# Column tiles for the recurrence's chunk products, whole rows for the sample's

## The chip, the cores and the metric

The kernel runs on one core of one Trainium2 chip. The core has a matrix engine (TensorE, PE in the profile, with PEld its weight loads), three others that compute (VectorE or DVE, ScalarE or ACT, GpSimd or POOL) and an engine that issues DMAs (SyncE or SP). The metric is the device time of one execution in microseconds (us), lower is better. Every product of two matrices reads a stationary operand (the weights) that is loaded into TensorE's array of 128 rows by 128 columns, and a moving operand that streams past it; a shape such as 128*32 in the profile names the rows and columns of the array that a product uses.

## The reference, cut to what matters

One layer of a streaming encoder over 2048 prompt frames and 64 frames of a running stream (the sample). Half of the width is chunked attention (8 heads of 64), half a gated linear recurrence, HGRN2 (4 heads of 128); each half is gated, both are joined, projected, added to the input and normalised.

```python
aq, ak, av, ag, hq, hf, hi, hg = jnp.split(rms_norm(x, ln_g) @ w_in, SPLITS, axis=-1)
o_a = attn_fn(heads(aq), k, v).reshape(B, T, W_A) * jax.nn.silu(ag)
o_b, S = hgrn2_branch(hq, hf, hi, hg, lb, norm_g, s0)
y = x + jnp.concatenate([o_a, o_b], axis=-1) @ w_out
```

The recurrence works by blocks. With b the running sum of the logarithms of the forget gates:

```python
qt = qb * jnp.exp(b)
kt = kb * jnp.exp(-b)
A = jnp.where(mask, jnp.einsum('bthk,bshk->bhts', qt, kt), 0.0)
o = jnp.einsum('bthk,bhkv->bthv', qt, S) + jnp.einsum('bhts,bshv->bthv', A, vb)
S = jnp.exp(bl)[..., None] * S + jnp.einsum('bshk,bshv->bhkv', kb * jnp.exp(bl[:, None] - b), vb)
```

Everything is float32; the outputs are both streams' results, the newest keys and values, and the recurrence's states.

## The kernel before, in words

The frames are worked off in four super-blocks of 512 columns; the second has 576, the last 64 of them the sample (SUPER, L38). For each super-block TensorE projects 32 groups of 128 features from the normalised input (project, L539; results in PSUM tiles `acc`, weights in `w`). Four of eight kinds of groups feed four pairs of attention heads (pair_jobs, L759), four feed four recurrence heads (head_jobs, L1248).

The order of the instructions on all engines is written out by a planner at build time (class Plan, L52). Each piece of work is a thread that yields what it waits for: a time, a token for a buffer (Tok), or a condition. The planner keeps a clock, C.now, which every product advances by an assumed cost (L132: 10 + 1.66 n ns for an fp32 product of n moving columns, marked slow); the other engines have a time at which they are free. The main thread emits the projections, two products at a time; between them whatever thread is ready emits its instructions. The engines then run their own instructions in that order and wait for one another by semaphores. All transfers are issued by SP.

**The recurrence** (rec_block, L1362) takes a block of a head's columns: 512, or in the second super-block first 256 and then 320, so there are 12 blocks of four chunks of 128 columns, four of two chunks, and four of two chunks and a sample chunk of 64. A chunk consists of blocks of 32 columns. Exponentials scale queries and keys relative to the middle of their block of 32 (q0, k0), to its start or end (q1, k1), or to the middle of the chunk (q2, k2), so that each is in range. The products inside a chunk (L1497 to L1508) write one PSUM tile `g`, keys by queries: k0 with q0, 128 by 128, which is right on the diagonal blocks of 32; then k1 of blocks 0 and 2 with q1 of blocks 1 and 3, 32 by 32; then k2 of blocks 0 and 1 with q2 of blocks 2 and 3, 64 by 64. Later ones overwrite what is not wanted of the earlier ones. VectorE copies what the mask keeps into `asb` (L1513), whose other entries stay zero. After that come the state update (kv, L1545: turned keys kn with the values iv), the states (L1567, L1569), and the output (og, L1580: iv with A, and the state before with qh, L1583). The sample's chunk has 64 rows, so those products use 64 rows of iv, kn and A. The products are fp32; TensorE executes each as two records.

**The sample's attention** (sample_a, L1161): five blocks of keys, four from the cache (vc) and one of 64 new ones (v); the probabilities of both heads are turned and split into two parts (split_p, L976: ScalarE copies, VectorE subtracts) in tiles `ph`, and ten products write `pv`. The tile `v` holds two heads, nine blocks of 128 keys; block 8 is the sample's, 64 rows of it used.

**The last pair's values** (ev_v_last, L835, in the last super-block): the projected values are turned by TensorE for each head of the pair, four transposes of 64 rows each, once that head's half of `v` is open (open_, L772; a half opens when the pair before has ended with it).

Of the kernel before, what the change touches and what calls it, by code (L numbers as in the profile page):

```python
# [17 lines left out]
P = 128  # L18
# [3 lines left out]
DEC = 64  # L22
# [161 lines left out]
def hymba_step(  # L184
# [574 lines left out]
    def pair_jobs(sb, p):  # L759
# [12 lines left out]
        def open_(h):  # L772

            yield from tk[f"kv{h}"].get()
            if "kd" not in room:
                room["kd"] = T(pa, [P, 2, WIN + NMAX], F32R, "kd")
                room["v"] = T(pa, [P, 2, 9, 2, 64], F32R, "v")
                room["q"] = T(pa, [P, 2, QW], F32R, "q")
            d.kd, d.v, d.q = room["kd"], room["v"], room["q"]
            if sb:  # L780
                cd = carry[sb - 1][p]
                sp.dma_start(f32(d.kd[:, h, 0:512]), cd[:, h])
                d.k_t[h] = C.dma(256)
                sp.dma_start(f32(d.v[:, h, 0:4].rearrange("p t s d -> p (t s d)")), cd[:, 2 + h])
                d.v_t[h] = C.dma(256)
            d.open[h] = True
            C.spawn(load_bias(sb, p, d, h), 1)
# [47 lines left out]
        def ev_v_last(acc, off, bn, t):  # L835
            yield from tk["vT"].get()
            yield "A", t
            vt = T(wk, [P, 512], F32, "vT", bufs=VTB)
            act.copy(vt[:, :bn], acc)
            t = C.act(bn, t)  # L840
            tk["acc"].put(1, t)
            nt = bn // P
            for h in range(2):
                yield lambda: d.open[h]
                yield from tk["tr"].get()
                yield t
                pt = tr_ps()
                for j in range(nt):
                    transpose(pt[:, j * 64 : j * 64 + 64], vt[own[h], j * P : (j + 1) * P], ident[own[h], own[h]])
                yield "A", C.pe()  # L850
                s3 = pt[:, : nt * 64].rearrange("p (t d) -> p t d", d=64)
                hi, lo = (d.v[:, h, 4 + off // P : 4 + off // P + nt, x] for x in (h, 1 - h))
                act.copy(hi, s3)
                t = C.act(nt * 64)
                yield "D", t
                dve.tensor_sub(lo, s3, f32(hi))
                t = C.dve(nt * 64, t)
                tk["tr"].put(1, t)
                d.v_n[h] += bn
                d.v_t[h] = max(d.v_t[h], t + 500.0)  # L860
            yield from new_rows(vt, off, bn, p, nv_prompt, None, tk["vT"], t)
            all_in()

# [297 lines left out]
    def sample_a(d, c0, marks):  # L1161
        yield lambda: d.left == [1, 1]
        yield lambda: d.cache is not None and all(x >= c0 + DEC for x in d.q_n + d.k_n + d.v_n)
        yield "D", max(d.q_t + d.k_t + d.v_t)
        q, kd, v, p = d.q, d.kd, d.v, d.p
        kc, vc = d.cache


        spans = [(kc, 0, 512), (kd, 512 + c0, DEC)]

        z = c0 + DEC
        for part in (q, ql):
            dve.memset(f32(part[:, :, z : z + DEC]), 0.0)
            dve.tensor_copy(part[:, 1, z + DEC : z + 2 * DEC], f32(part[:, 1, c0:z]))
        t = C.dve(500)
        yield t
        yield from tk["s_ps"].get()
        yield from tk["pr"].get()
        sps = s_ps()
        for i, (ks, k0, kn) in enumerate(spans):  # L1180
            for part in (q, ql):
                for h in range(2):
                    a = (c0, z)[h]
                    mm(sps[:, i, :kn], part[:, h, a : a + P], ks[:, h, k0 : k0 + kn], kn,
                       start=part is q and h == 0, stop=part is ql and h == 1)
        t = C.pe()
        yield "D", t
        s = T(wk, [P, 640], F32, "pr", bufs=PRB)
        nm = T(wk, [P, 2], F32, "nm", bufs=4)
        for h in range(2):  # L1190
            hs = own[h]
            for i, kn in enumerate((512, DEC)):
                dve.tensor_tensor_reduce(s[hs, i * 512 : i * 512 + kn], sps[hs, i, :kn],
                                         d.bias[hs, h, 64 * h + i * 512 : 64 * h + i * 512 + kn],
                                         1.0, 3e38, ALU.add, ALU.min, nm[hs, i : i + 1])
                t = C.dve(kn, t)
        dve.tensor_tensor(nm[:, 0:1], nm[:, 0:1], nm[:, 1:2], ALU.min)
        t = C.dve(10, t)
        tk["s_ps"].put(1, t)
        for h in range(2):  # L1200
            d.left[h] -= 1
            tk[f"bias{h}"].put()
        yield "A", t
        out = []
        yield from softmax_exp(s, nm, 576, out, t)
        pr, t = out[0]
        yield lambda: marks[-1]["pv"] and turn["ph"] == turn["given"]
        yield t + 300.0
        phs = []
        for j0, nj, kr in ((0, 4, P), (4, 1, DEC)):  # L1210
            yield from tk["tr"].get()
            pt = tr_ps()
            for j in range(j0, j0 + nj):
                transpose(pt[:kr, (j - j0) * P : (j - j0 + 1) * P], pr[:, j * P : j * P + kr], ident)
            t = C.pe()
            if j0:
                tk["pr"].put(1, t)
            yield "A", t
            yield from tk["ph"].get()
            ph = T(wk, [P, 2, 512], F32R, "ph", bufs=2)  # L1220
            t = yield from split_p(pt, ph, kr, nj * P, t)
            tk["tr"].put(1, t)
            phs.append(ph)
        yield t + 200.0
        yield from tk["mixa"].get()
        mix = T(wk, [P, 256], F32, "mixa", bufs=2)
        yield from tk["pv"].get()
        pv = psum("pv").rearrange("p (h s q) -> p h s q", h=2, s=2)[:, :, :, :DEC]
        for h in range(2):
            for j in range(5):  # L1230
                kr = P if j < 4 else DEC
                cc = (j % 4) * P + h * DEC
                mm(pv[:, h], vcols(vc, j, h, kr) if j < 4 else vcols(v, 4 + c0 // P, h, kr), phs[j // 4][:kr, :, cc : cc + DEC], P,
                   start=(j == 0), stop=(j == 4))
        tk["ph"].put(2, C.pe())
        t = C.pe()
        yield "A", t
        for h in range(2):
            t = yield from finish_pv(h, pv[:, h], mix, DEC, t)
        tk["pv"].put(1, t)  # L1240
        tk["raw"].put(2)
        C.spawn(mix_out(d, mix, c0, DEC, t, True), 1)
# [5 lines left out]
    def head_jobs(sb, h):  # L1248
# [65 lines left out]
        def ifree():  # L1314
            if r.gi is None:
                if tk["gi"].n == 0:
                    return False
                tk["gi"].take()
                r.gi = True
                r.iv = T(pg, [P, 5 * P], F32, "gi")  # L1320
            return True

        def qd():
# [26 lines left out]
    def recurrence(r):  # L1350
        sb, h = r.sb, r.h
        t0, n, blocks = SUPER[sb][:3]
        for bi, (off, bn) in enumerate(blocks):
# [4 lines left out]
            yield from rec_block(r, off, bn, lastb)  # L1358
            tk["rec"].put()
        tk["gi"].put()  # L1360

    def rec_block(r, off, bn, lastb):  # L1362
        sb, h = r.sb, r.h
# [130 lines left out]
        yield td  # L1494
        yield from tk["g"].get()
        ag = bank()
        for i, (cc, nbk, smp) in enumerate(chunks):  # L1497
            w = nbk * 32
            mm(ag[:w, i, :w], k0[:, cc : cc + w], q0[:, cc : cc + w], w, True, start=True, stop=True)
        yield None  # L1500
        for i, (cc, nbk, smp) in enumerate(chunks):
            for j in range(0, nbk, 2):
                a, b = cc + 32 * j, cc + 32 * j + 32
                mm(ag[32 * j : 32 * j + 32, i, 32 * j + 32 : 32 * j + 64],
                   k1[:, a : a + 32], q1[:, b : b + 32], 32, start=True, stop=True)
        for i in range(nprc):
            mm(ag[0:64, i, 64:128], k2[:, i].rearrange("p j t -> p (j t)"),
               q2[:, i].rearrange("p j t -> p (j t)"), 150, start=True, stop=True)  # L1508
        t = C.pe()
        yield "D", t  # L1510
        for cs, w in merged():
# [4 lines left out]
        if by_dma:  # L1516
# [6 lines left out]
                         kh[:, :full].rearrange("p (a c j) -> p c a j", a=4, j=32))  # L1523
            if bn > full:
                act.copy(kn[:DEC, nprc], kh[:DEC, full : full + P])
            t = C.act(bn, rows["t"])
            yield t + 200.0
        else:
# [7 lines left out]
            kn = tmp("k1").rearrange("p (c t) -> p c t", t=P)  # L1536
            for cs, w in merged():
                act.copy(kn[:w, cs], tg[:w, cs])
            t = C.act(bn, t)
            yield t + 200.0  # L1540
        kv = bank()
        iv = r.iv
        for i, (cc, nbk, smp) in enumerate(chunks):
            w = nbk * 32
            mm(kv[:, i], kn[:w, i], iv[:w, off + cc : off + cc + P], P, True, start=True, stop=True)  # L1545
        t = C.pe()
        yield "D", t
        before = []
# [28 lines left out]
        og = bank()  # L1577
        for i, (cc, nbk, smp) in enumerate(chunks):
            w = nbk * 32
            mm(og[:, i, :w], iv[:w, off + cc : off + cc + P], A[:w, i, :w], P, True,  # L1580
               start=True, stop=before[i] is None)
            if before[i] is not None:
                mm(og[:, i, :w], before[i], qh[:, cc : cc + w], P, True, start=False, stop=True)  # L1583
# [673 lines left out]
```

## Time and profile before

| | |
|---|---|
| median of 3 runs | 1241.81 us (1240.01 to 1243.0) |
| the profiled execution's own time | 1241.93 us |
| its span in the profile | 1240.2 us |
| TensorE busy | 1228.5 us (99%), 7398 records |
| VectorE, ScalarE, GpSimd busy | 893.8, 680.3, 417.3 us |
| granted clock of TensorE | 0.999 |

A row of a group names line, engine, operation, tiles (out<-in), shape, count, then busy time and the mean duration of one, then idle time before it. A row of the timeline has the start in us, the time from the first start to the last end of the merged instructions, and their count; where instructions of several shapes of one line and the same tiles follow one another, one row holds them all under the first one's shape. A window's rows hold the records that fall into it. A matmul's duration is a latency, and records overlap; the distance of starts tells what one costs.

### The profile page before, as it was taken

Reading aid. Unit: us, or ns where it says so; the run is one execution under the profiler, and the core shown is the slowest. Engines: PE = TensorE matmul, PEld = TensorE weight load, DVE = VectorE, ACT = ScalarE, POOL = GpSimd, SP = SyncE. Lnnn points to the kernel's source line nnn. Section 1 sums busy time; section 2 is a strip of 40 time slices with the busy share of each in tenths; the row PEclk is TensorE's granted clock in tenths of the full one; section 3 lists DMA queues with packets and bytes.
Section 4 is the critical chain, followed back from the end, with each engine's and each line's share of the span. In section 5 each row is a group of like instructions: output and inputs, shape, how many; then the busy total and the mean of one; then the engine's idle time right before and its main releaser. Section 6 shows DMA issues by size and latency. Waiting matters only on the chain.

```text
span 1240.2 us, 21233 instructions
## 1 busy us (share of the span) xinstructions
PE 1228.5 (99%) x7398; PEld 1078.9 (87%) x7398; DVE 893.8 (72%) x1897; ACT 680.3 (55%) x1526; POOL 417.3 (34%) x702
## 2 busy tenths in 40 slices
PE   9999999999999999999999999999999999999997
PEld 7888888999999999998888888988888888788786
DVE  7687878777767677687587667785768566867775
ACT  6354546655565547574465556664646445644443
POOL 7665565111120111201242242133342202665543
PEclk9999999999999999999999999999999999999999
DMA  8897979667575476555787878678888686988431
GB/s 339 302 319 256 328 281 343 205 179 242 159 221 156 150 238 210 193 167 187 265 270 253 300 241 282 227 238 276 261 275 262 222 251 212 336 260 252 131 136 68
DMA packets 158324, 294.36 MB, mean 237 GB/s; under 512 B 51657, under 2 KB 98377, under 8 KB 140554
## 3 DMA queue, kind: packets, MB, share of 16 engines
q1 hardware_dynamic: 157784, 292.74, 70.7%
q8 instruction: 58, 0.95, 0.3%
q14 instruction: 48, 0.39, 0.1%
q10 hardware_dynamic: 434, 0.27, 0.1%
HBM read 198.52 MB, written 95.49 MB: 237 GB/s over the span
## 4 chain that ended last, share of the span: by engine, by line
PE 90%; DMA 5%; DVE 2%; ACT 1%; SPq 1%; issue 0%; POOL 0%; ACTq 0%; DVEq 0%; POOLq 0%
PE acc L249 58%; PE g L249 9%; PE pv L249 7%; PE tr L253 6%; PE s L249 5%; PE tr L249 4%; DMA vT<-way 2%; DMA w<-wd 2%; DMA way<-vT 1%; DMA out_dram<-ck 1%; PE g L253 1%; DMA bias<-wind 0%; DVE pr L948 0%; SPq L711 0%; SPq L1684 0%
## 5 line engine op out<-in xcount | busy, mean ns | idle before, releaser
L249 PE MATMUL acc<-xh,w 128*128 128x512 f32 (+2 forms) x2720 | 564.5, 347 | 0.6 <-ACT xh L409 0.5
L249 PEld LDWEIGHTS acc<-xh,w 128*128 128x128 f32 x2720 | 435.7, 189 | 51.5 <-ACT xh L409 0.9
L249 PE MATMUL acc<-xl,w 128*128 128x512 f32 (+2 forms) x1360 | 291.4, 346 | 0.2 <-DVE xl L415 0.2
L249 PEld LDWEIGHTS acc<-xl,w 128*128 128x128 f32 x1360 | 220.5, 189 | 26.2 <-DVE xl L415 0.4
L948 DVE CUSTOM_DVE_ANT_0 pr<-s,bias 128x640 f32<-128x640 f32 (+4 forms) x128 | 94.2, 736 | 53.6 <-PE s L249 53.1
L965 ACT ACTIVATE pr<-pr,nm 128x640 f32<-128x640 f32 (+4 forms) x132 | 100.3, 760 | 52.8 <-DVE nm L948 52.5
L977 ACT CAST ph<-tr 128x512 fp32r<-128x512 f32 (+3 forms) x176 | 87.8, 506 | 74.5 <-PE pv L249 45.5
L473 POOL TENSOR_TENSOR w<-wraw,w 128x256 fp32r<-128x256 f32 x120 | 102.3, 881 | 55.6 <-DVE w L468 40.5
L980 DVE TENSOR_TENSOR ph<-tr,ph 128x512 fp32r<-128x512 f32 (+3 forms) x176 | 100.7, 587 | 21.6 <-ACT ph L977 21.0
L249 PE MATMUL pv<-ph,v 128*128 128x256 f32 (+2 forms) x344 | 97.8, 371 | 0.9 <-DVE ph L980 0.6
L253 PE MATMUL tr<-ident,pr 128*128 128x128 f32 x580 | 88.2, 273 | 0.5 <-DVE sm L968 0.5
L1596 POOL TENSOR_TENSOR k<-ob 128x512 f32<-128x512 f32 (+2 forms) x20 | 18.0, 902 | 200.3 <-ACT ob L1587 162.3
L510 POOL TENSOR_TENSOR xn<-wraw,xn 128x256 fp32r<-128x256 f32 x48 | 40.6, 848 | 132.1 <-ACT xn L507 127.1
L1121 POOL TENSOR_TENSOR mixa<-mixa,sga 128x256 f32<-128x256 f32 (+1 forms) x36 | 28.6, 793 | 167.9 <-DVE mixa L1019 142.2
L969 DVE TENSOR_SCALAR pr<-pr,sm 128x640 f32<-128x640 f32 (+4 forms) x132 | 76.2, 577 | 4.7
L1019 DVE TENSOR_TENSOR mixa<-mixa,pv 64x256 f32<-64x256 f32 (+1 forms) x144 | 56.8, 394 | 31.0 <-ACT mixa L1015 27.3
L253 PEld LDWEIGHTS tr<-ident,pr 128*128 128x128 f32 x580 | 69.8, 140 | 10.3 <-PE tr L253 0.9
L575 ACT ACTIVATE sig<-acc 128x512 f32<-128x512 f32 (+2 forms) x63 | 31.8, 505 | 72.8 <-PE acc L249 72.1
L249 PEld LDWEIGHTS pv<-ph,v 128*128 128x128 f32 (+1 forms) x344 | 58.2, 189 | 9.8 <-DVE ph L980 1.4
L1015 ACT COPY mixa<-pv 64x256 f32<-64x256 f32 (+1 forms) x72 | 25.1, 349 | 59.4 <-PE pv L249 53.3
L249 PE MATMUL s<-kd,q 128*128 128x320 f32 (+2 forms) x232 | 55.8, 311 | 0.2 <-DVE nm L948 0.2
L249 PE MATMUL s<-kd,ql 128*128 128x320 f32 (+2 forms) x232 | 55.5, 309 | 0.0
(415 smaller groups left out, 2122.5 us busy)
## 6 DMA issues: line engine op xcount, KB each, us to landing
w<-wd SPq DMA_DIRECT2D x96, 1024.0 KB, 5.8
wd<-w SPq DMA_DIRECT2D x32, 1024.0 KB, 7.4
wraw<-in_w_in_dram SPq DMA_DIRECT2D x30, 512.0 KB, 5.4
wod<-xn SPq DMA_DIRECT2D x28, 512.0 KB, 5.8
xn<-in_x_prompt_dram SPq DMA_DIRECT2D x23, 512.0 KB, 4.8
bias<-biasd SPq DMA_DIRECT2D x24, 320.0 KB, 5.5
carry<-kd SPq DMA_DIRECT2D x12, 512.0 KB, 6.2
carry<-v SPq DMA_DIRECT2D x12, 512.0 KB, 6.4
```

The source lines that it names most:

```text
L249: pe.matmul(out, w, x, **kw)
L253: pe.transpose(out, x, idn)
L473: pool.tensor_sub(w[:, 1, k : k + 2], raw[:, k : k + 2], f32(w[:, 0, k : k + 2]))
L510: pool.tensor_sub(f32r(st[:, c.start + 512 : c.stop + 512]), src[:, c], st[:, c])
L575: act.activation(sig[:, :bn], acc, AF.Exp, scale=-1.0)
L948: dve.tensor_tensor_reduce(s[:, :nk].rearrange("p (a c) -> p a c", a=ns), sps[:, :ns, :kn], d.bias[:, h, bcol : bcol + nk].rearrange("p (a ...
L965: act.activation(s[:, :nk], s[:, :nk], AF.Exp, bias=nm[:, 0:1], scale=-1.0, accum_out=sm)
L969: dve.tensor_scalar(s[:, :nk], s[:, :nk], sm, None, ALU.mult)
L977: act.copy(ph[:krows, 0, :wid], pt[:krows, :wid])
L980: dve.tensor_sub(ph[:krows, 1, :wid], pt[:krows, :wid], f32(ph[:krows, 0, :wid]))
L1019: dve.tensor_add(mix[hs, :qn], mix[hs, :qn], pv[hs, i, :qn])
L1121: pool.tensor_mul(mix[:, :n], mix[:, :n], d.sg[:, g0 : g0 + n])
```

## The change

The products inside a chunk are all made 32 columns of the array wide (block_mm), at the array's columns where their 32 rows of output lie. The product of k0 and q0 is cut into one product for each block of 32 keys, with the queries up to that block's end; k2 of blocks 0 and 1 becomes two products of 32 keys by 64 queries. The planner's thread no longer yields between them, and its clock is advanced by 250 ns and by those products alone whose keys are block 0. The sample's state update, output, and attention values use all 128 rows; what lies beyond 64 in kn, iv, v and ph is set to zero by GpSimd (A's rows there are zero at those columns before). The last pair's values are turned with all 128 rows in four transposes, after the second half is open, and each head takes its columns from the result.

```diff
--- before.py
+++ after.py
@@ -775,6 +775,7 @@
             if "kd" not in room:
                 room["kd"] = T(pa, [P, 2, WIN + NMAX], F32R, "kd")
                 room["v"] = T(pa, [P, 2, 9, 2, 64], F32R, "v")
+                pool.memset(f32(room["v"][DEC:, :, 8]), 0.0)
                 room["q"] = T(pa, [P, 2, QW], F32R, "q")
             d.kd, d.v, d.q = room["kd"], room["v"], room["q"]
             if sb:
@@ -840,24 +841,25 @@
             t = C.act(bn, t)
             tk["acc"].put(1, t)
             nt = bn // P
+            yield lambda: d.open[1]
+            yield from tk["tr"].get()
+            yield t
+            pt = tr_ps()
+            for j in range(nt):
+                transpose(pt[:, j * P : j * P + P], vt[:, j * P : (j + 1) * P], ident)
+            t = C.pe()
             for h in range(2):
-                yield lambda: d.open[h]
-                yield from tk["tr"].get()
-                yield t
-                pt = tr_ps()
-                for j in range(nt):
-                    transpose(pt[:, j * 64 : j * 64 + 64], vt[own[h], j * P : (j + 1) * P], ident[own[h], own[h]])
-                yield "A", C.pe()
-                s3 = pt[:, : nt * 64].rearrange("p (t d) -> p t d", d=64)
+                yield "A", t
+                s3 = pt[:, : nt * P].rearrange("p (t h d) -> p t h d", h=2, d=64)[:, :, h]
                 hi, lo = (d.v[:, h, 4 + off // P : 4 + off // P + nt, x] for x in (h, 1 - h))
                 act.copy(hi, s3)
                 t = C.act(nt * 64)
                 yield "D", t
                 dve.tensor_sub(lo, s3, f32(hi))
                 t = C.dve(nt * 64, t)
-                tk["tr"].put(1, t)
                 d.v_n[h] += bn
                 d.v_t[h] = max(d.v_t[h], t + 500.0)
+            tk["tr"].put(1, t)
             yield from new_rows(vt, off, bn, p, nv_prompt, None, tk["vT"], t)
             all_in()
 
@@ -1218,6 +1220,8 @@
             yield "A", t
             yield from tk["ph"].get()
             ph = T(wk, [P, 2, 512], F32R, "ph", bufs=2)
+            if kr < P:
+                pool.memset(f32(ph[kr:, :, : nj * P]), 0.0)
             t = yield from split_p(pt, ph, kr, nj * P, t)
             tk["tr"].put(1, t)
             phs.append(ph)
@@ -1228,9 +1232,8 @@
         pv = psum("pv").rearrange("p (h s q) -> p h s q", h=2, s=2)[:, :, :, :DEC]
         for h in range(2):
             for j in range(5):
-                kr = P if j < 4 else DEC
                 cc = (j % 4) * P + h * DEC
-                mm(pv[:, h], vcols(vc, j, h, kr) if j < 4 else vcols(v, 4 + c0 // P, h, kr), phs[j // 4][:kr, :, cc : cc + DEC], P,
+                mm(pv[:, h], vcols(vc, j, h, P) if j < 4 else vcols(v, 4 + c0 // P, h, P), phs[j // 4][:, :, cc : cc + DEC], P,
                    start=(j == 0), stop=(j == 4))
         tk["ph"].put(2, C.pe())
         t = C.pe()
@@ -1318,6 +1321,8 @@
                 tk["gi"].take()
                 r.gi = True
                 r.iv = T(pg, [P, 5 * P], F32, "gi")
+                if SUPER[sb][1] > WIN:
+                    pool.memset(r.iv[DEC:, WIN : WIN + P], 0.0)
             return True
 
         def qd():
@@ -1358,6 +1363,12 @@
             yield from rec_block(r, off, bn, lastb)
             tk["rec"].put()
         tk["gi"].put()
+
+    def block_mm(ag, i, j, col, keys, queries):
+        n = queries.shape[-1]
+        pe.matmul(ag[32 * j : 32 * j + 32, i, col : col + n], keys, queries, start=True, stop=True)
+        if j == 0:
+            C.now += 10.0 + 1.66 * n
 
     def rec_block(r, off, bn, lastb):
         sb, h = r.sb, r.h
@@ -1494,18 +1505,19 @@
         yield td
         yield from tk["g"].get()
         ag = bank()
+        C.now += 250.0
         for i, (cc, nbk, smp) in enumerate(chunks):
-            w = nbk * 32
-            mm(ag[:w, i, :w], k0[:, cc : cc + w], q0[:, cc : cc + w], w, True, start=True, stop=True)
-        yield None
-        for i, (cc, nbk, smp) in enumerate(chunks):
+            def k_(x, j):
+                return x[:, cc + 32 * j : cc + 32 * j + 32]
+
+            for j in range(nbk - 1, 0, -1):
+                block_mm(ag, i, j, 0, k_(k0, j), q0[:, cc : cc + 32 * j + 32])
+            if nbk == 4:
+                for j in range(2):
+                    block_mm(ag, i, j, 64, k2[:, i, j], q2[:, i].rearrange("p j t -> p (j t)"))
             for j in range(0, nbk, 2):
-                a, b = cc + 32 * j, cc + 32 * j + 32
-                mm(ag[32 * j : 32 * j + 32, i, 32 * j + 32 : 32 * j + 64],
-                   k1[:, a : a + 32], q1[:, b : b + 32], 32, start=True, stop=True)
-        for i in range(nprc):
-            mm(ag[0:64, i, 64:128], k2[:, i].rearrange("p j t -> p (j t)"),
-               q2[:, i].rearrange("p j t -> p (j t)"), 150, start=True, stop=True)
+                block_mm(ag, i, j, 32 * j + 32, k_(k1, j), k_(q1, j + 1))
+            block_mm(ag, i, 0, 0, k_(k0, 0), k_(q0, 0))
         t = C.pe()
         yield "D", t
         for cs, w in merged():
@@ -1523,6 +1535,7 @@
                          kh[:, :full].rearrange("p (a c j) -> p c a j", a=4, j=32))
             if bn > full:
                 act.copy(kn[:DEC, nprc], kh[:DEC, full : full + P])
+                pool.memset(kn[DEC:, nprc], 0.0)
             t = C.act(bn, rows["t"])
             yield t + 200.0
         else:
@@ -1536,13 +1549,15 @@
             kn = tmp("k1").rearrange("p (c t) -> p c t", t=P)
             for cs, w in merged():
                 act.copy(kn[:w, cs], tg[:w, cs])
+                if w < P:
+                    pool.memset(kn[w:, cs], 0.0)
             t = C.act(bn, t)
             yield t + 200.0
         kv = bank()
         iv = r.iv
         for i, (cc, nbk, smp) in enumerate(chunks):
             w = nbk * 32
-            mm(kv[:, i], kn[:w, i], iv[:w, off + cc : off + cc + P], P, True, start=True, stop=True)
+            mm(kv[:, i], kn[:, i], iv[:, off + cc : off + cc + P], P, True, start=True, stop=True)
         t = C.pe()
         yield "D", t
         before = []
@@ -1577,7 +1592,7 @@
         og = bank()
         for i, (cc, nbk, smp) in enumerate(chunks):
             w = nbk * 32
-            mm(og[:, i, :w], iv[:w, off + cc : off + cc + P], A[:w, i, :w], P, True,
+            mm(og[:, i, :w], iv[:, off + cc : off + cc + P], A[:, i, :w], P, True,
                start=True, stop=before[i] is None)
             if before[i] is not None:
                 mm(og[:, i, :w], before[i], qh[:, cc : cc + w], P, True, start=False, stop=True)
```

## The prediction

> **What bounds the kernel now.** I read the page first (busy time and the chain of work that ended last), then the waits of TensorE, then TensorE's groups by shape, then its timeline around each place that the change touches.
>
> ```profile
> PE 1228.5 (99%) x7398; PEld 1078.9 (87%) x7398; DVE 893.8 (72%) x1897; ACT 680.3 (55%) x1526; POOL 417.3 (34%) x702
> PE 90%; DMA 5%; DVE 2%; ACT 1%; SPq 1%; issue 0%; POOL 0%; ACTq 0%; DVEq 0%; POOLq 0%
> ...
> PE acc L249 <- DMA w<-wod: 1.1, 1, 1.1
> PE pv L249 <- DVE ph L980: 0.6, 1, 0.6
> ```
>
> TensorE is busy for 1228.5 of 1240.2 us and is 90% of the chain; of the 11.7 us that it is idle, the largest single wait in mid-kernel is 1.1 us. Its order is fixed and it has no slack, so a nanosecond taken from TensorE's stream comes off the end, unless a producer is then late. Every step below is therefore priced in TensorE time.
>
> ```profile
> L249 PE MATMUL g<-q,k 128*128 128x128 f32 x128 | 17.5, 274 | 0.0
> L249 PE MATMUL g<-q,k 128*64 128x64 f32 x136 | 13.0, 230 | 0.0
> L249 PE MATMUL g<-q,k 128*32 128x32 f32 x264 | 8.1, 199 | 0.0
> ```
>
> These are the products inside a chunk: rows*columns of the array, then the moving columns. An fp32 product is two records (64 chunks give the 128 wide ones; 64 chunks of two products and 4 sample chunks of one give 132, so 264 narrow ones). The means are latencies; what a record costs is the step from start to start.
>
> **The change, part 1: the products inside a chunk.** One recurrence block of 512 columns (four chunks), and the same records in narrower windows:
>
> ```profile
> 45.28 0.61 PE L249 MATMUL acc<-xh,w 128*128 128x512 f32 x2
> 45.74 1.05 PE L249 MATMUL g<-q,k 128*128 128x128 f32 x8
> 46.54 0.71 PE L249 MATMUL acc<-xh,w 128*128 128x512 f32 x2
> 47.19 1.05 PE L249 MATMUL g<-q,k 128*32 128x32 f32 x24
> 48.17 1.19 PE L249 MATMUL acc<-xh,w 128*128 128x512 f32 x4
> ...
> 45.74 0.94 PE L249 MATMUL g<-q,k 128*128 128x128 f32 x7
> 47.19 0.45 PE L249 MATMUL g<-q,k 128*32 128x32 f32 x16
> 47.73 0.51 PE L249 MATMUL g<-q,k 128*64 128x64 f32 x6
> ```
>
> (The row of 24 is 16 records of 32 columns and then 8 of 64.) Price of the block before: from 45.28 to the end at 49.36 are 4.08 us. Eight projection records alone would take 7 steps of 0.23 and one latency of 0.39, 2.00. The block costs 2.08 us.
>
> Step per record, (time - latency)/(count - 1): 128 columns (0.94 - 0.274)/6 = 0.111; 64 columns (0.51 - 0.222)/5 = 0.058. Both lie on 0.005 + 0.00083 per column, which gives 0.085 for 96 and 0.0315 for 32. But the 32-column records step by (0.45 - 0.20)/15 = 0.0167, half of that. Those products alternate between the array's columns 0 to 31 and 64 to 95 (keys of blocks 0 and 2), so two column tiles run at once, at no loss.
>
> Changing the width costs too. In: the projection record before 47.19 starts at 46.54 + 0.71 - 0.40 = 46.85, so 0.33 instead of 0.23: 0.10. Out: the last 64-column record starts at 47.73 + 0.51 - 0.22 = 48.02, and 48.17 is 0.15 later instead of 0.06; the four records after it take (1.19 - 0.39) = 0.80 for three steps instead of 0.69. Together 0.20.
>
> After: all products of a chunk are 32 columns wide, in four tiles. By the diff, tile 0 gets moving columns of 64 + 32 + 32, tile 1 64 + 64, tile 2 96 + 32, tile 3 128: 128 each. With two records a product, tile 0 takes 2 x (0.058 + 0.0315 + 0.0315) = 0.242 us, tile 1 0.232, tile 2 0.233, tile 3 0.222. Four tiles at once occur nowhere in this trace. Bounds: each at its own pace, 0.242 us a chunk; or one record at a time, the sum, 0.929. I take 0.242, since the nearest row shows two tiles at once without loss. A block is then 4 x 0.242 + 0.30 for one change in and out + 0.07 for filling and emptying the tiles (the first record's weights 0.03, and tile 0's first product is the fourth in order) = 1.34. Saved: 0.74 a block, 12 blocks: 8.9 us.
>
> A block of two chunks now costs 2.08 less two chunks of 2 x 0.111 + 4 x 0.0157 + 2 x 0.058 = 0.40, 1.28; after, 2 x 0.242 + 0.37 = 0.85. Saved 0.43, four blocks: 1.7 us. The block with the sample chunk:
>
> ```profile
> 289.51 0.88 PE L249 MATMUL acc<-xl,w 128*128 128x256 f32 x6
> 290.23 0.87 PE L249 MATMUL g<-q,k 128*128 128x128 f32 x6
> 291.02 0.50 PE L249 MATMUL acc<-xl,w 128*128 128x256 f32 x2
> 291.46 0.75 PE L249 MATMUL g<-q,k 128*32 128x32 f32 x14
> 292.14 1.37 PE L249 MATMUL acc<-xh,w 128*128 128x256 f32 x9
> ```
>
> From 289.51 to 293.51 are 4.00 us; 17 projection records at steps of 0.12 ((0.88 - 0.28)/5) and one latency are 2.20, so it costs 1.80: the sample's 64-wide product adds a further pair of width changes. After, 0.85 + 0.126 for tile 0 of the sample chunk = 0.98. Saved 0.82, four times: 3.3 us.
>
> **Part 2: the 64-row products over 128 rows.** State update, output and attention values of the sample:
>
> ```profile
> 301.94 1.02 PE L249 MATMUL g<-gi,k 128*128 128x128 f32 x6
> 302.89 0.30 PE L253 MATMUL tr<-ident,vT 128*64 128x128 f32 x1
> 302.95 0.82 PE L249 MATMUL acc<-xh,w 128*128 128x320 f32 x4
> ...
> 310.80 0.39 PE L249 MATMUL g<-bm,S 128*128 128x128 f32 x2
> 311.11 0.43 PE L249 MATMUL g<-asb,gi 64*128 64x64 f32 x2
> 311.48 0.43 PE L249 MATMUL g<-bm,So 128*128 128x64 f32 x2
> 311.75 0.61 PE L253 MATMUL tr<-ident,pr 128*128 128x128 f32 x4
> ...
> 353.14 0.56 PE L249 MATMUL pv<-ph,wraw 128*128 128x128 f32 x4
> 353.63 0.32 PE L249 MATMUL pv<-ph,v 64*128 64x128 f32 x1
> 353.88 0.66 PE L249 MATMUL pv<-ph,wraw 128*128 128x128 f32 x4
> 354.48 0.32 PE L249 MATMUL pv<-ph,v 64*128 64x128 f32 x1
> 354.73 0.71 PE L249 MATMUL g<-gi,k 128*128 128x128 f32 x4
> ```
>
> State update: 301.94 to 303.77 is 1.83. At whole-array steps it would be 6 x 0.111 + 0.11 + 3 x 0.147 + 0.31 = 1.53 (0.147 for 320 columns lies between the 0.12 of 256 and the 0.23 of 512): 0.30 saved (the row of six hides that its last two are 64-row records). Output: 310.80 to 311.75 is 0.95 for six records, 0.67 at 0.111: 0.28. Values: 353.14 to 355.44 is 2.30; ten records and the four after them would take 0.06 + 9 x 0.111 + 3 x 0.111 + 0.275 = 1.67: 0.63. Four heads or pairs each: 1.2 + 1.1 + 2.5 = 4.8 us.
>
> The zeros cost memsets on GpSimd: one for v at the start, four each of ph, iv and kn, 13 in all. The trace has none of their size; the nearest rows:
>
> ```profile
> L1416 POOL MEMSET sf<- 128x16 f32 x20 | 2.2, 110 | 0.0
> L473 POOL TENSOR_TENSOR w<-wraw,w 128x256 fp32r<-128x256 f32 x120 | 102.3, 881 | 55.6 <-DVE w L468 40.5
> L1121 POOL TENSOR_TENSOR mixa<-mixa,sga 128x256 f32<-128x256 f32 (+1 forms) x13 | 9.4, 720 | 90.1 <-DVE mixa L1019 67.7 <-DMA way<-vT 12.1 <-issue 10.3
> ```
>
> Between 0.11 and 0.88 us each (128 or 256 elements), 1.4 to 11 us on an engine that is busy a third of the time; nothing on TensorE if they are done before the copies and subtractions of the same tiles by ScalarE and VectorE, which cover them. kn and ph are new waits of TensorE, with its whole stream queued behind: 8 places. Uncovered, 0 to 0.88 each, up to 7 us; I take 0.6 in all.
>
> **Part 3: the last pair's values.** Twice four 64-row transposes become four whole ones:
>
> ```profile
> 1051.02 0.84 PE L249 MATMUL acc<-xl,w 128*128 128x512 f32 x3
> 1051.79 0.46 PE L253 MATMUL tr<-ident,vT 64*128 64x64 f32 x4
> 1052.18 0.56 PE L249 MATMUL s<-kd,q 128*128 128x320 f32 x2
> ...
> 1068.00 0.48 PE L249 MATMUL pv<-ph,v 128*128 128x512 f32 x1
> ```
>
> The last projection record starts at 1051.47, so 1052.18 is 0.48 later than its own step allows, and the next record loses 0.10: 0.58 a half, 1.16 for both. After: 4 x 0.11 = 0.44. Saved 0.7. The first half, which now is turned with the second, comes some 12 us later, but the last pair's first value product is at 1068.00, and the wait is one of the planner, which lets other work go ahead; I cost it at nothing. No DMA is added, and no queue is passed.
>
> **Sum.** 8.9 + 1.7 + 3.3 + 4.8 + 0.7 - 0.6 = 18.8 us from the profiled execution's own 1241.93 (0.12 over the median of 1241.81): 1223.1. The planner's clock also changes: it charged 4 x 222.5 + 8 x 63 + 4 x 259 = 2430 ns for a block of 2.08 us, and now 250 + 4 x 242 = 1220 for 1.34. A clock that ran ahead of the chip there no longer does, so consumers are placed rather later than earlier; that speaks for few new stalls.
>
> **Rivals.** (a) Products start in program order. Then only the second record of a product overlaps the first of the next, and a chunk takes 0.111 + 0.085 + 3 x 0.058 + 3 x 0.0315 + 8 x 0.007 (the gap inside an overlapped pair) = 0.52. Blocks: 2.45, 1.41 and 1.57; lost 4.4 and 0.5, saved 0.9, and with 4.9 elsewhere 1241. Against it: in order, eight products of 32 columns would spread their starts over about 0.30 us, and the row of 16 shows 0.25, as with two free tiles. The Trainium skill, "TensorE: Matmul & The Clock Gate", Part 3, The mechanism, states this rule: matmuls are strict FIFO, in program order. This case's 16 records disagree.
>
> (b) Two tiles at once is all that the array's input gives: 0.929/2 = 0.465 a chunk, blocks of 2.23, 1.30 and 1.43, net saving 4.5, 1237. The trace can't exclude it.
>
> (c) Slower: with four tiles addressed the records run one at a time, 0.93 a chunk. Place: the 64 chunks' bursts; it decides from 0.242 + 18.8/64 = 0.54 a chunk on. Blocks of 4.09, 2.23 and 2.47: 24.1 + 3.8 + 2.7 lost, 4.9 kept, 1268. Against it stands the same row of 16.
>
> (d) The zeros are late: a memset stands in GpSimd's queue behind the multiply of L1121, which waited 67.7/13 = 5.2 us each for VectorE. Eight times 0.5 to 3 us lost: 1227 to 1247. Against it: GpSimd is in order by the planner's time, and what that multiply waits for precedes the sample's product on TensorE too.
>
> **Numbers.** Forecast 0.70 (own range 1219 to 1228), (b) 0.10, (a) 0.07, (c) 0.05, (d) and other late producers 0.08. From 1217, for blocks that fill and empty faster, to 1238, which takes in (b) and most of (d). A measurement of this kernel tells about 0.2%, 2.5 us, from no change: faster 0.70 + 0.10 + 0.02 of (a) + 0.04 of (d) = 0.86; same 0.06; slower 0.08.
>
> **What would show it.** One burst of 64 records (32 columns wide) for a four-chunk block, spanning about 1.2 us with its last latency; over 1.9 says (b) or (a), near 3.9 (c). No 64-row record but those of the sample's input rows (from xn), which the change leaves. TensorE's busy time near 1210. Waits of TensorE on GpSimd, lines of memset, over 2 us say (d). If TensorE's busy time falls by 18 and the span doesn't, a producer or DMA has become the bound, and my first step was wrong.

## The result: faster by about half of the forecast

The changed kernel takes 1230.95 us, median of four runs (1229.05 to 1236.85), against 1241.63 beside it. The ratio is 0.9922, with a 95% interval of 0.9903 to 0.9940: 9.7 us faster (7.4 to 12); the two medians are 10.7 us apart. The forecast was 18.8 us. The direction is right, and the prediction's range of 1217 to 1238 holds the time; the narrower one that it gave for its own mechanism, 1219 to 1228, doesn't.

Below is the page of the changed kernel's profiled execution, which took 1236.85 us and is the slowest of the four, so it shows more waiting than the median lost:

```profile
span 1234.9 us, 22287 instructions
PE 1213.7 (98%) x7914; PEld 1069.1 (87%) x7914; DVE 897.7 (73%) x1897; ACT 678.9 (55%) x1526; POOL 416.2 (34%) x715
PE 85%; DMA 9%; ACT 2%; DVE 1%; SPq 1%; issue 1%; POOL 0%; ACTq 0%; POOLq 0%; DVEq 0%
```

TensorE is busy 14.8 us less, but it is idle for 1234.9 - 1213.7 = 21.2 us, where it was 11.7. DMA has grown from 5% to 9% of the chain of work that ended last. Its longest waits:

```profile
PE g L249 <- ACT k L1534: 3.8, 2, 3.4
PE g L253 <- DVE xn L382: 3.3, 1, 3.3
PE tr L253 <- DVE ph L982: 1.7, 2, 0.9
PE pv L249 <- DVE ph L982: 1.6, 2, 1.0
```

TensorE has no wait on GpSimd but the one at the start of the program. Two waits of over 3 us are new, at 240.5 and 905 us. What they do beyond their own length stands in stretches around them (columns: stretch, its length, busy time and records of TensorE, its weight loads, VectorE, ScalarE and GpSimd, then the granted clock, DMA share and GB/s):

```profile
240.00:245.00 5.00, 1.68 (x16) 1.43 (x16) 4.64 (x12) 2.98 (x10) 0.00 (x0) 1.00 0.83 311
245.50:248.80 3.30, 3.30 (x13) 3.24 (x13) 3.23 (x14) 2.54 (x10) 1.83 (x9) 0.50 0.13 50
900.00:908.00 8.00, 4.97 (x23) 3.76 (x21) 1.54 (x3) 1.24 (x4) 1.43 (x2) 0.98 0.94 311
908.40:914.40 6.00, 6.00 (x19) 5.23 (x20) 4.14 (x10) 2.48 (x6) 2.49 (x4) 0.50 0.49 151
914.50:920.00 5.50, 5.50 (x34) 4.81 (x33) 2.00 (x3) 2.60 (x5) 3.68 (x5) 1.00 0.59 176
```

After each wait the granted clock is 0.50 for 3 to 7 us: 19 records in 6 us, then 34 in 5.5. Over the whole span the clock is 0.995 where it was 0.999, and 0.004 of 1235 is 4.9 us, an estimate by the mean clock. So the profiled execution adds up: TensorE's work at full clock fell by about 14.8 + 4.9 = 19.7 us, 9.5 went into new waits and 4.9 into the slower clock after them, and 5.3 are left, its span's 1240.2 - 1234.9. The other executions vary: 1229.05 to 1232.49, at clocks of 0.994 to 0.997.

What ended the wait at 905 us stands one step further back. ScalarE's copy had itself waited 6.74 us, for a transfer of turned keys (bl from way) that goes through memory:

```profile
892.15 1.81 SPq L711 DMA_DIRECT2D way<-bl  x4
897.80 1.00 SPq L715 DMA_DIRECT2D bl<-way  x1
907.71 0.62 ACT L1534 COPY k<-bl 128x512 f32<-128x512 f32 x1 [6.74 <-DMA bl<-way]
```

Between its two halves the planner has placed five other transfers (kd, v, bias, w and wod), and from the issue of the second half to ScalarE's copy 9.9 us pass. In the kernel before, only wod stands between the halves of the same transfer and the others come behind it; 3.3 us pass there, and ScalarE has no wait:

```profile
898.35 1.84 SPq L711 DMA_DIRECT2D way<-bl  x4
901.99 0.34 SPq L715 DMA_DIRECT2D bl<-way  x1
905.26 0.62 ACT L1522 COPY k<-bl 128x512 f32<-128x512 f32 x1
```

The products inside a chunk, one block of 512 columns in the timeline, then the same burst in a window of its first 40 ns:

```profile
45.43 0.61 PE L249 MATMUL acc<-xh,w 128*128 128x512 f32 x2
45.98 1.16 PE L1369 MATMUL g<-q,k 128*32 128x128 f32 x64
47.06 1.43 PE L249 MATMUL acc<-xh,w 128*128 128x512 f32 x5
...
45.98 0.30 PE L1369 MATMUL g<-q,k 128*32 128x128 f32 x4
```

Four records start within 40 ns, of 128, 96, 64 and 64 columns: one in each tile, the first records of the first four products in the program's order. Their second records don't keep that order: in the trace those of 64 columns start at 46.07, the one of 96 at 46.09, and that of the first product, of 128, last, at 46.11. The 64 records start within 1.16 - 0.20 = 0.96 us, 0.24 a chunk. From 45.43 to 48.49 are 3.06 us; seven projection records alone take 6 x 0.23 + 0.39 = 1.77, so the block costs 1.29, where 1.34 was forecast.

The sample's attention values, whose 1.59 us for ten products (353.14 to 354.73 before) are now 1.06:

```profile
351.77 0.56 PE L249 MATMUL pv<-ph,wraw 128*128 128x128 f32 x4
352.16 0.28 PE L249 MATMUL pv<-ph,v 128*128 128x128 f32 x1
352.27 0.61 PE L249 MATMUL pv<-ph,wraw 128*128 128x128 f32 x4
352.72 0.27 PE L249 MATMUL pv<-ph,v 128*128 128x128 f32 x1
352.83 0.66 PE L249 MATMUL g<-gi,k 128*128 128x128 f32 x4
```

and the zeros, by GpSimd's groups:

```profile
L1224 POOL MEMSET ph<- 64x256 f32 x4 | 1.2, 307 | 12.7 <-PE pv L249 12.3 <-POOL k L1611 0.4
L1325 POOL MEMSET gi<- 64x128 f32 x4 | 1.0, 258 | 0.2
L1553 POOL MEMSET k<- 64x128 f32 x2 | 0.5, 232 | 14.9 <-PE g L1369 14.9
L1538 POOL MEMSET k<- 64x128 f32 x2 | 0.4, 199 | 4.1 <-PE g L1369 4.1
```

A zeroing costs 0.2 to 0.3 us, inside the bounds of 0.11 and 0.88, on an engine that nobody waited for there. The profile before had a row of this size, which the prediction passed over: one MEMSET of 128x128 (L281) at 204 ns.

### The profile page after: what moved, and what is told of

Read it like the earlier page. It is cut to its first block, busy times and chain, and to the rows that moved or that the text cites. A ratio compares the mean times of both kernels' runs of the same rounds, so it can differ in the third digit from the quotient of the medians.

```text
span 1234.9 us, 22287 instructions
## 1 busy us (share of the span) xinstructions
PE 1213.7 (98%) x7914; PEld 1069.1 (87%) x7914; DVE 897.7 (73%) x1897; ACT 678.9 (55%) x1526; POOL 416.2 (34%) x715
## 4 chain that ended last, share of the span: by engine, by line
PE 85%; DMA 9%; ACT 2%; DVE 1%; SPq 1%; issue 1%; POOL 0%; ACTq 0%; POOLq 0%; DVEq 0%
PE acc L249 56%; PE pv L249 7%; PE g L249 7%; PE tr L253 5%; PE s L249 5%; PE tr L249 4%; DMA vT<-way 1%; DMA bl<-way 1%; PE g L1369 1%; DMA w<-wd 1%; DMA ck<-in_cache_attn_v_dram 1%; DMA way<-vT 1%; DMA mixd<-ob 1%; DMA bias<-biasd 1%; DMA carry<-kd 1%
## 5 line engine op out<-in xcount | busy, mean ns | idle before, releaser
L249 PEld LDWEIGHTS acc<-xl,w 128*128 128x128 f32 x1360 | 223.3, 191 | 25.6
L971 DVE TENSOR_SCALAR pr<-pr,sm 128x640 f32<-128x640 f32 (+4 forms) x132 | 79.8, 604 | 4.7
L249 PEld LDWEIGHTS pv<-ph,v 128*128 128x128 f32 x344 | 59.2, 190 | 10.4 <-issue 1.4
L1017 ACT COPY mixa<-pv 64x256 f32<-64x256 f32 (+1 forms) x72 | 25.1, 349 | 60.3 <-PE pv L249 54.2
```

Of the source, the lines that this page charges most:

```text
L249: pe.matmul(out, w, x, **kw)
L971: dve.tensor_scalar(s[:, :nk], s[:, :nk], sm, None, ALU.mult)
```

## The experiments

The question is where 9.5 us of waits and 4.9 of clock come from: from the changed order of the instructions, from TensorE being faster in any order, or from how far the planner's clock departs from the chip's. The planner can be made to write one order with the products of the other kernel: it sees charges and pauses only. The letters M, O, W, P and V name theories, each explained in the recorded expectation that brings it in. The amount that the prediction gave for the old charge was misread. Only the four 128-column products carry the mark "slow"; those of 32 and 64 columns are charged 12 + n/2.37 ns, so a block of four chunks was charged 890 + 8 x 25.5 + 4 x 75 = 1395 ns, not 2430.

**The order of before, the new products.** In the changed kernel, the charge of before takes the place of the new one:

```diff
-        if j == 0:
-            C.now += 10.0 + 1.66 * n
...
-        C.now += 250.0
+        for cc, nbk, smp in chunks:
+            C.mm(nbk * 32, True)
+        yield None
+        for cc, nbk, smp in chunks:
+            for j in range(0, nbk, 2):
+                C.mm(32)
+        for i in range(nprc):
+            C.mm(150)
```

> The changed kernel, with the planner charging for the products inside a chunk what it charged before (1395 ns for a block of four chunks, with the old pause of its thread): up to the last pair's values TensorE's order of all other work is that of before, and the products are the new ones, all in one burst at the place of the old second one. Structure saves the same 19 us of TensorE as the change. Theory M (margin: TensorE waits where the planner's clock no longer lags behind the chip; here it charges 1.40 us for 1.29, so no lag): TensorE idle 18 to 25 us, time 1228 to 1234. Theory O (the changed order by itself has worse places, whatever the clock): idle near the 12 us of before, 1221 to 1225. Theory W (a faster TensorE leaves producers late in any order): 1228 to 1234, as M.

Measured: 1230.28 us, ratio 0.9901 (0.9882 to 0.9920). TensorE busy 1210.4 of a span of 1227.7: 17.3 idle. That is within M's and W's 1228 to 1234 and over O's; the idle time is a little under M's. Of its six waits of 0.7 us and more, four fall between 1036 and 1057 us, where the turning of the last pair's values changes the order once more.

**The order of after, the old products.** In the kernel before, the products keep their form, and the charge is the new one:

```diff
-            mm(ag[:w, i, :w], k0[:, cc : cc + w], q0[:, cc : cc + w], w, True, start=True, stop=True)
-        yield None
+            pe.matmul(ag[:w, i, :w], k0[:, cc : cc + w], q0[:, cc : cc + w], start=True, stop=True)
+            for n in (64, 32, 32) if nbk == 4 else (32, 32):
+                C.mm(n, True)
```

(250 ns are added ahead, and the other products are no longer charged.)

> The kernel before (old products, 64-row products, old turning of the last pair's values), with the planner charging the new amounts (1220 ns for a block of four chunks that takes 2.08 us), so that up to the last pair's values TensorE's order of all other work is that of the change. Theory M: the clock lags 0.86 us a block, more than before: idle 12 us or less, 1238 to 1242. Theory O: the order brings its waits along, idle near 21 us: 1249 to 1256. Theory W: 1240 to 1242.

Measured: 1253.02 us, ratio 1.0094 (1.0079 to 1.0109). Busy 1230.0 of 1251.2, 21.2 idle. The time is as O says; that the idle time is just that of the change is chance. Up to the last pair's values, where the two orders part, TensorE idles for 8.4 us here and 13.5 in the change, behind them for 6.2 and 1.1 (and 6.7 at the end of the program in both). Its waits:

```profile
PE g L253 <- DVE xn L382: 3.0, 1, 3.0
PE s L249 <- DVE nm L948: 2.8, 1, 2.8
PE pv L249 <- ACT ph L977: 1.6, 1, 1.6
...
PE g L249 <- ACT k L1524: 1.3, 1, 1.3
```

The wait for xn is the one of the change, at 244 instead of 241 us, and the one for k (L1524 here, L1534 there) has come along too; the transfer behind it follows the same five others, and ScalarE waits 4.6 us for it. M is out: this kernel's planner lags furthest behind the chip, and yet it waits far more than before. W can't be all either, since nothing in this kernel is faster. What the order does at 241 us can be read in VectorE's timeline in the change:

```profile
240.87 0.28 DVE L683 TENSOR_TENSOR v<-vT,v 128x128 fp32r<-128x128 f32 x1
241.07 0.68 DVE L415 TENSOR_TENSOR xl<-tr,xh 128x512 fp32r<-128x512 f32 x1
242.07 0.42 DVE L580 TENSOR_TENSOR gq<-acc,sig 128x256 f32<-128x256 f32 x1 [0.32 <-ACT sig L577]
242.42 1.27 DVE L382 SCALAR_TENSOR_TENSOR xn<-xn,rstd,gin 64x1024 f32<-64x1024 f32 x1
```

In TensorE's order the transposes of the sample's input rows come next, while VectorE, busy for 2.9 of these 3.3 us, does other things before it scales these rows (the last line). In the kernel before, VectorE scaled them earlier, and their transposes came at 243.40 without a wait:

```profile
239.97 1.27 DVE L382 SCALAR_TENSOR_TENSOR xn<-xn,rstd,gin 64x1024 f32<-64x1024 f32 x1
```

**The charge alone, lower and higher.**

```diff
-        C.now += 250.0
+        C.now += -380.0
```

> The changed kernel with one number altered: the planner's clock is advanced by -380 ns instead of +250 ns before a block's products, so it charges 0.59 us for a burst of 1.29 and lags by 0.7 us a block, as the kernel before did (1.40 for 2.08). Theory M: idle back to about 12 us, 1221 to 1226. Theory O: a new order with its own luck, anywhere from 1222 to 1236. Theory W: 1228 to 1234.

Measured: 1245.99 us, ratio 1.0036 (1.0020 to 1.0051); busy 1212.1 of 1242.9, 30.8 idle. M said 1221 to 1226 and falls here too; it is worse than any of the three expected. With +1000.0 in the same place:

> As e5_charge_low with +1000 ns: 1.97 us charged for a burst of 1.29, so the planner's clock runs 0.7 us a block ahead of the chip. Theory M: more waits than the change, idle over 28 us, 1236 to 1245. Theory O: anywhere from 1222 to 1236, not ordered by the charge. Theory W: 1228 to 1234.

Measured: 1229.54 us, ratio 0.9903 (0.9884 to 0.9922); busy 1210.2 of 1227.2, 17.0 idle. M's 1236 to 1245 is refuted; the time is no different from the change's. Which side of the chip's time the charge lies on doesn't order the times.

**The parts alone.** The column tiles and their charge put into the kernel before, with the 64-row products and the old turning of values:

> The kernel before with the column tiles and their planner charge alone: 64-row products and the old turning of the last pair's values stay. TensorE's order of all other work is that of the change up to the last pair's values. Structure (the steps of the sum): 13.9 us less TensorE work than before, 5.5 more than the change. Theory O (most of the loss is made by the order's places): the waits of the change come along, 1234 to 1239. Theory W (waits grow with the TensorE time that is taken away, 0.35 us for each us): 1241.8 - 13.9 x 0.65 = 1233, 1231 to 1235.

Measured: 1245.61 us, ratio 1.0038 (1.0021 to 1.0054), slower than before and above both expectations. Its busy time is 1220.5 of 1244.8, 24.3 idle, at a clock of 0.992, the lowest but two of the profiled executions. The places of this order stand again among its waits, and one of 4.2 us near the end, for nm, which e2_order_of_after had too and the change has not:

```profile
PE s L249 <- DVE nm L948: 4.2, 1, 4.2
PE g L253 <- DVE xn L382: 3.5, 1, 3.5
PE g L249 <- ACT k L1529: 2.7, 2, 2.4
```

The sample's whole rows and the whole transposes, with the old products and their charge:

> The changed kernel with the old products inside a chunk and their old planner charge: only the sample's whole rows with their zeros and the last pair's whole transposes are new. TensorE's order is that of before up to the last pair's values. Structure: 5.5 us less TensorE work than before. If the zeros come in time, no wait of TensorE on GpSimd and 1235.5 to 1237.5; if they are late, a wait at the sample's four state updates and four value products, over 1238. Theory W: 1241.8 - 5.5 x 0.65 = 1238.2.

Measured: 1239.46 us, ratio 0.9982 (0.9973 to 0.9992). Busy 1222.4, 6.1 less than before (5.5 forecast), and 14.8 idle. No wait on GpSimd, so late zeros are out; 3 us of waits have come instead, 2.3 of them one wait of transposes near 1068 us for VectorE's part of ph. That is over what the zeros in time gave (1235.5 to 1237.5), and over W's 1238.2 too.

**All consumers later.** In the changed kernel, the planner's allowance after each instruction of the other engines:

```diff
-        return start + ns + 150.0
+        return start + ns + 700.0
```

> The changed kernel with the planner's allowance after each instruction of ScalarE, VectorE and GpSimd raised from 150 to 700 ns, so that whatever uses a result is placed later in TensorE's order (TensorE's work is unchanged). Theory W (producers are late for a faster TensorE by fractions of a microsecond): the short waits go, idle inside the order under 6 us, 1220 to 1226. Theory O (each order has its own few bad places): a new order, 1222 to 1240, no better on average. A third, P: later consumers lengthen the recurrence's and attention's chains, and the waits move to the ends of the super-blocks: over 1232.

Measured: 1283.24 us, ratio 1.0347 (1.0328 to 1.0367); busy 1227.2 of 1281.4, 54.2 idle, clock 0.985. The time is as P says. The longest wait, by the timeline:

```profile
546.59 0.87 PE L249 MATMUL s<-kd,q 128*128 128x320 f32 x2 [8.06 <-DMA kd<-carry]
```

It is near a super-block's end, and the profile names the transfer of keys from memory as what ended it; others of 5.1 and 1.9 us stand at 822 and 843. These three are 15 of the 54.2 us; many of the others lie inside the super-blocks, so P's mechanism accounts for a part only. With the higher charge as well:

> As e9_later_consumers with the charge of e6_charge_high (+1000 ns in place of +250). Theory W: 1219 to 1225. Theory O: anywhere from 1222 to 1240. Theory P: over 1232, by waits at the ends of the super-blocks.

Measured: 1287.92 us, ratio 1.0381 (1.0363 to 1.0400), 54.7 idle: P again. W's remedy, later consumers, is wrong by 60 us. With an allowance of 50 instead:

> The changed kernel with the planner's allowance after each instruction of ScalarE, VectorE and GpSimd lowered from 150 to 50 ns, the other side of e9_later_consumers (700 ns: 1283 us). Theory P, if the time goes steadily with the allowance: 9.5 us per 100 ns over 150, so 1219 to 1227. Theory W (results that are late by fractions of a microsecond make the waits): more short waits, 1233 to 1240. Theory O: a new order, anywhere from 1226 to 1246.

Measured: ratio 0.9905 (0.9885 to 0.9924), median 1232.46 us; one of its four executions took 4260.54 us, for a reason that the record doesn't show, the others 1230.26 to 1234.58. Idle 20.6. P's steady course ends at 150 ns, and W's 1233 to 1240 is not reached by two of three; O's wide 1226 to 1246 holds, as it would hold most results.

**The order of before to the very end.** As the first experiment, with the old turning of the last pair's values put back:

```diff
-            yield lambda: d.open[1]
...
-                transpose(pt[:, j * P : j * P + P], vt[:, j * P : (j + 1) * P], ident)
+                yield lambda: d.open[h]
...
+                    transpose(pt[:, j * 64 : j * 64 + 64], vt[own[h], j * P : (j + 1) * P], ident[own[h], own[h]])
```

> e1_order_of_before with the last pair's values turned as before, in two times four 64-row transposes: TensorE's order of everything but the products inside a chunk is now that of before to the end. Structure: 0.7 us more TensorE work than e1. Theory V (turning the values together, later for the first half, reorders the end and makes the waits that e1 and e4 show between 1036 and 1068 us): idle inside the order 4.5 to 6 us, 1224 to 1228. Theory W (a faster TensorE makes the waits): idle 8 to 10 us as in e1, 1230 to 1232.

Measured: 1226.64 us, ratio 0.9881 (0.9866 to 0.9895). This interval lies below the change's (0.9903 to 0.9940): the version beats both kernels. (It overlaps that of e1_order_of_before, 0.9882 to 0.9920.) In its trace all of TensorE's records but those of the products inside a chunk, and all of VectorE's, stand in the very order of before. Its page and its longest waits behind the one at the start:

```profile
span 1223.6 us, 22301 instructions
PE 1209.5 (99%) x7918; PEld 1064.0 (87%) x7918; DVE 895.3 (73%) x1897; ACT 680.9 (56%) x1526; POOL 421.8 (34%) x715
```

```profile
PE g L249 <- DVE So L1576: 1.4, 1, 1.4
PE pv L249 <- DVE ph L981: 1.0, 2, 0.6
PE pv L249 <- DVE sm L969: 1.0, 1, 1.0
```

TensorE's busy time is 19.0 us under that of before, and no wait in its order is longer than 1.4 us; the clock is 0.999. Idle is 14.1, 2.4 more than before: in this order that is all that W accounts for. V's 1224 to 1228 holds. The next one leaves the products inside a chunk as before too:

> The kernel before with the sample's products over 128 rows with zeros alone; the order of before to the end. Structure: 4.8 us less TensorE work. Theory V: idle 3.5 to 4.5 us as before, 1236 to 1237.5, below the 1239.5 of e4_rows_alone, which also turns the values whole. Theory W: idle 5 us or more, 1238 to 1239.5.

(The kernel before, with the sample's whole rows and their zeros alone.) Measured: 1235.96 us, ratio 0.9957 (0.9942 to 0.9972). Busy 1223.2, 5.3 less than before, where 4.8 was forecast. V again: without the whole transposes it is 3.5 us faster than with them (e4_rows_alone). And with the higher charge in place of the old one:

> e6_charge_high with the old turning of the last pair's values. Theory V: 1 to 3 us below e6's 1229.5, 1226 to 1229. Theory W, and O if the end of this order had no bad place: 1229.5 to 1231.

Measured: 1235.85 us, ratio 0.9947 (0.9930 to 0.9964), 6.3 us slower than with the whole transposes, and 23.1 idle. V is not general: the old turning helps in the order of before and hurts in this one. It is again the order that its place in the plan brings about.

## Why the prediction was right, and where its size was off

**TensorE as the bound, and the structure.** Right. The new products alone make the difference between f2_zeros_alone's busy time, 1223.2, and f1_whole_order_of_before's, 1209.5: 13.7 us, where 8.9 + 1.7 + 3.3 = 13.9 was the sum. The zeros were worth 5.3 (4.8 forecast), and the busy time of the change, at full clock, is about 19.7 us lower (19.4 was the sum without the 0.6 for late zeros).

**Four tiles at once.** Right, at 0.24 us a chunk. Rivals (a), 0.52, (b), 0.465, and (c), 0.93, are refuted by the burst's 0.96 us for four chunks. The rule of the Trainium skill, "TensorE: Matmul & The Clock Gate", Part 3, The mechanism, that matmuls start in program order, doesn't hold across column tiles here: of the second records, those of 64 columns start first and that of the first product, of 128, last. The prediction's count against rival (a), from the row of 16, took it that the two records of a product stand next to each other in the program; the burst needs no such premise.

**Zeros that are late, rival (d).** Refuted in its mechanism: no wait on GpSimd in the change or in either kernel with the zeros alone.

**New waits, put at nothing.** This step failed. The 0.6 us in the sum stood for late zeros, which made no wait; for any other wait of TensorE the sum had no term, on the ground that the planner's new clock "speaks for few new stalls". Measured in its place, in the profiled execution: 9.5 us of waits, and about 4.9 of clock after them. In part it is the sign that the prediction named last: TensorE's busy time fell by 14.8 us and the span by 5.3. The ground, that the old charge ran ahead of the chip and the new one doesn't, was wrong in its number (1395, not 2430 ns for 2.08 us: it lagged by 0.69), and also as a rule, since neither a lagging nor a leading clock orders the times of the experiments.

What the runs show instead: a changed charge, or a removed pause, gives a new order of the instructions of all engines, and each of the other orders that were tried waits more than that of before, as far as one profiled execution of each tells. The kernel before has 11.7 us of idle time, the lowest of all; with its order to the end it stays at 13.1 and 14.1, in all others it is 14.8 to 54.7. Order and products can be told apart up to the last pair's values, behind which the orders part once more. TensorE's idle time up to there:

| | old products | new products |
|---|---|---|
| order of before | 2.7 us (before) | 5.4 us (f1_whole_order_of_before) |
| order of the change | 8.4 us (e2_order_of_after) | 13.5 us (the change) |

So the changed order costs 5.7 us with the old products and 8.1 with the new, and the faster products cost 2.7 us in the old order and 5.1 in the new: theory W has a part, and the two together cost more than their sum. (The new products are here the column tiles and the sample's whole rows; the column tiles alone, e3_tiles_alone, idle 10.5 us in the order of the change.) Behind that place the change idles 1.2 us less than before. For the two longest, the rows show the place: VectorE's scaling at 241 us has moved behind other work, and the transfer at 898 us behind five others.

**The last pair's whole transposes.** Half right: 0.7 us of TensorE are saved (e4_rows_alone is busy 0.8 less than f2_zeros_alone), but "nothing" for the later first half was too little: in the order of before they cost 3.5 us net (e4_rows_alone against f2_zeros_alone), by what is re-planned after them; in another order they gained 6.3 (e6_charge_high against f3_high_old_values).

**The time.** 1223.1 was the structure with next to no new waits; f1_whole_order_of_before, which comes near to that, takes 1226.64, 4.3 us less than the change. That the range of 1217 to 1238 holds 1230.95 is in part luck: it was made so wide for rivals (b) and (d), and both are refuted, while what took the time was in no term. Left open: what makes one order better than another. That VectorE's queue or a DMA is late at a place can be read each time, but no rule for the planner's constants was found, and the readings at 241 and 905 us are arguments from the timeline, not experiments that moved one wait. Nor was it tried to hold TensorE's order and take such a wait away.

## What to carry to other kernels

When the bounding engine has 1% of slack in an order that a planner wrote, a change of the work and a change of the plan are two changes: price the second by itself, and where possible keep the old order (by keeping the old charges) while the instructions are replaced. An estimate from the engine's steps can be right within 1 us and still lose half to waits. Look also at the order in which the transfers are issued: one that the bounding engine needs soon can end up behind others that have time. And here it paid to spread products of 32 output rows over all four column tiles, balanced by their moving columns, even though more than a third of what they compute (192 of 512 moving columns a chunk) is thrown away.

## What the runs showed of the hardware that was not expected

Waits can cost more than their length. In the change, TensorE's clock is 0.50 for 3 to 7 us after a wait of over 3 us, as in the stretches shown. The kernel with the higher charge shows it after a wait of 2.4 us too (columns: stretch, length, TensorE busy and records, granted clock, DMA share, GB/s):

```profile
870.00:877.00 7.00, 7.00 (x37) 1.00 0.93 271
877.00:880.00 3.00, 0.60 (x3) 1.00 1.02 429
881.20:884.40 3.20, 3.20 (x10) 0.54 0.78 263
885.00:890.00 5.00, 5.00 (x28) 1.00 0.74 267
```

Ten records in 3.2 us stand against 28 in 5. Below 3 us length alone doesn't decide: after waits of 2.3 us (e4_rows_alone, at 1068 us), 2.4 (e3_tiles_alone, 907) and 2.8 (e2_order_of_after, 1077) the clock stayed at 1.00, while all waits of 2.9 us and more in these profiles were followed by a stretch at 0.50. Waits of 0.5 to 1.4 us, as in f1_whole_order_of_before, left its clock at 0.999. The runs of the change lie further apart, 1229.05 to 1236.85, than those of f1_whole_order_of_before, 1225.28 to 1228.52, which has no long wait; that the clock makes this difference was not tested.
